# Moving the key-weight reads of layer 0's second output sweep to other weight tiles

## The chip, the cores and the metric

The kernel runs on one core of a Trainium2 chip. The metric is the device time of one execution in microseconds (us); it is the median of several runs. One further execution was recorded by the hardware profiler, and every row of a profile or trace below is from that one. Times inside the trace are counted from the start of its span.

## The reference

The program is a two-layer diffusion transformer with 256 tokens of `x` and 256 context tokens of `ctx`, model width 2048 and branch width 4096. All inputs are float32. Cut to what matters here:

```python
for i in range(2):
    shift, scale, gate = split(silu(c) @ ada_w[i] + ada_b[i], 3)          # modulation of x
    shift_c, scale_c, gate_c = split(silu(c_ctx) @ ada_w[i] + ada_b[i], 3) # modulation of ctx
    h  = rmsnorm(x,  norm_g[i]) * (1 + scale)   + shift
    hc = rmsnorm(xc, norm_g[i]) * (1 + scale_c) + shift_c
    y, yc = fourier_branch(h), fourier_branch(hc)      if i == 0
    y     = attention_branch(h, hc)                    if i == 1
    x  = x  + gate   * (y  @ w_out[i])
    xc = xc + gate_c * (yc @ w_out[i])                 # layer 0 only
return rmsnorm(x, final_g)
```

The stage of interest is the last product of layer 0, `y @ w_out[0]` for both token sets, a 512 x 4096 by 4096 x 2048 product. Beside it, and on other engines, the modulation of layer 1 (`silu(c) @ ada_w[1]`) and sums of squares of weights of layer 1 are computed.

## The kernel before, in words

**The output loop.** Lines 1028 to 1080 run `for i in range(32)`: two sweeps of 16 weight tiles, `sw = i // 16` and `kg = i % 16`. Sweep 0 makes the first half of the output columns, sweep 1 (the second sweep, tiles 16 to 31) the other half. For each i one 1 MB weight tile `raw` comes through SyncE's DMA queue (SP) from `in_wo`, three buffers deep. `split16` (L137, L138) makes of each half j of `raw` one fp16 pair `wf`: ScalarE (ACT) writes the high part (L137), VectorE (DVE) the remainder (L138). TensorE (PE) then runs 48 matmuls, three per block (L145, L146, L147): L145 and L146 read the high part, L147 the remainder that DVE wrote. Tiles with kg 14 and 15 go through `ws_split` (L66, L67) in place of it. PE begins the loop near 658 us of the trace, the first sweep ends near 826 and the second near 1000.

**The six weight buffers.** The pool with tag `ws` has six slots of 512 KB. The `wf` halves and the `wa` tiles of the modulation share them, so a new `wa` or `wf` takes the slot of whichever of them comes free, and its DMA or ACT instruction waits for the last reader of the tile that stood there.

**The modulation steps.** `next(ada)` (L784 to L795) is one step: a 512 KB tile `zr` of `ada_w` through SP's queue (L787, two buffers) and a 512 KB tile `wa` through POOL's queue (L790, in the `ws` pool), each multiplied on DVE with the activated condition `cb` and summed (L792). A step of a modulation with both token sets has two DVE passes for each tile, the first into a scratch tile `junk` and the second in place; one of x alone has one. `ada_rate` gives the number of steps per weight tile: two for i from 6 to 9 and from 17 to 25, none for 14, 15, 16 and from 28, else one.

**The pieces.** `scan_loads` (until i = 13) and `scan_loads1` read pieces of other weights on POOL's queue, two DMAs of 256 KB a piece (L834 for `in_wo`, L819 for `in_wkv`, the key weights of layer 1). `scan_sums` squares and sums what has been read, on ACT (L827). There are 16 key-weight pieces, 32 DMAs; all must be summed before `h1_bound` at i = 28 uses the sum.

**What sets the order.** The loop names the work, and each engine's instructions are then put in one fixed order when the program is built: an instruction that is ready early by the scheduler's reckoning may be put ahead of one named earlier. At run time every engine takes its instructions strictly in that order, so that one that waits holds up all behind it. DVE does the `wf` remainders, the modulation passes and, in the first sweep, `y_split0` (L894) in one such queue; POOL issues the `wa`, `in_wkv`, `in_wo` and `in_xT` transfers in one.

Of the kernel before, what the change touches and what calls it, by code (L numbers as in the profile page):

```python
# [32 lines left out]
def tile_dit(ctx: ExitStack, tc: tile.TileContext, a: dict, out: bass.AP):  # L33
# [10 lines left out]
    def psum():  # L44
        return pp.tile([P, 512], F32, tag="ps", name="ps")

    def raw(src, q=None):
        t = rawp.tile([P, D], F32, tag="raw", name="raw")
        n = src.shape[-1]
        last_dma[0] = (q or nc.sync).dma_start(t[:, :n], src).ins  # L50
        return t
# [3 lines left out]
    def act(dt=F32):  # L55
        return actp.tile([P, 512], dt, tag="act", name="act")
# [77 lines left out]
    def split16(t, i, up):  # L134
        w = wsp.tile([P, 2, 1024], F16, tag="ws", name="wf")
        src = t[:, i * 1024 : (i + 1) * 1024]
        last_cast[0] = S.activation(w[:, 0], src, AF.Copy, scale=up).ins  # L137
        last_sub[0] = V.scalar_tensor_tensor(w[:, 1], src, up, w[:, 0], op0=ALU.mult, op1=ALU.subtract).ins  # L138
        return w[:, 0], w[:, 1]

    def ws_split(t):
        return [half_split(t, i) for i in range(2)]
# [671 lines left out]
    def scan_loads1(n):  # L814
        for j in [next(scans1) for _ in range(n)]:
            for q in range(2):
                t = act()
                c = (j % 2 * 2 + q) * 512
                nc.gpsimd.dma_start(t, a["wkv"][j // 2][:, c : c + 512])  # L819
                c = j * 2 + q  # L820
                c += 80 if c < 28 else -28
                pend.append((t, scn[:, c : c + 1]))

    def scan_sums():
        while pend:
            t, c = pend.pop(0)
            S.activation(t, t, AF.Square, accum_out=c)  # L827

    def scan_loads(n):
        for j in [next(scans) for _ in range(n)]:  # L830
            for q in range(2):
                t = act()
                c = (j % 2 * 2 + q) * 512
                nc.gpsimd.dma_start(t, a["wo0"][j // 32, j % 32 // 2][:, c : c + 512])  # L834
                c = j * 2 + q - 64 * (j >= 40)
                pend.append((t, scn[:, c : c + 1]))
# [5 lines left out]
    def half_sum(sw):  # L842
        return [col_sum(scn[:, sw * 16 : sw * 16 + 64])] + [col_sum(scn[:, 80:108])] * (sw == 0)

    def half_scale(sw, sums_):
        x, up = sum_scale(sums_[0])
        if sw == 0:
            xy, uy = sum_scale(sums_[1])
            keep(ysc[:, 0:1].bitcast(I32), xy)
            keep(ysc[:, 1:2], uy)  # L850
        up_ = keep(ysc[:, 2 + 3 * sw : 3 + 3 * sw], up)
        both, dn = ysc[:, 3 + 3 * sw : 4 + 3 * sw], ysc[:, 4 + 3 * sw : 5 + 3 * sw]
        V.tensor_tensor(both, up_, ysc[:, 1:2], op=ALU.mult)
        V.tensor_scalar(dn.bitcast(I32), x, ysc[:, 0:1].bitcast(I32), -27.0 * 2**23, op0=ALU.add, op1=ALU.add)
        return up_, both, dn

    with tc.tile_pool(name="yp", reuse_waits="tile", bufs=32) as ypool:
# [23 lines left out]
        def y_split0(i):  # L881
            for j in range(2):
                k = i % 16 * 2 + j
                if k < 28:
                    if i < 16:
                        t = (ypool if k > 1 else actp).tile([P, 1024], F16, tag="y" if k > 1 else "act", name="y")
                        h, l, up = t[:, 0:512], t[:, 512:1024], ysc[:, 1:2]
                    else:
                        yy[i, j] = yy[i - 16, j]
                        continue  # L890
                else:
                    h, l, up = act(F32R), act(F32R), osc[i // 16][1]
                last_cast[0] = S.activation(h, ys[k], AF.Copy, scale=up).ins
                last_sub[0] = V.scalar_tensor_tensor(l, ys[k], up, h if k < 28 else h.bitcast(F32), op0=ALU.mult, op1=ALU.subtract).ins  # L894
                yy[i, j] = (h, l)
# [108 lines left out]
        def h1_bound():  # L1004
            m, c = h_bound(gs1, sh1, False), tiny(F32, 4, "t4")
            V.tensor_copy(c[:, 0:1], m)
            for i, q in ((2, slice(80, 108)), (3, slice(0, 4))):
                V.tensor_reduce(c[:, i : i + 1], scn[:, q], axis=AX.X, op=ALU.add)
            V.tensor_tensor(c[:, 1:2], c[:, 2:3], c[:, 3:4], op=ALU.add)
            nc.gpsimd.dma_start(hbd, c[:, 0:2])  # L1010
            hb1.append(act())
            nc.gpsimd.dma_start(hb1[0][:, 0:N], hbd.rearrange("(o p) c -> o (p c)", o=1).broadcast_to([P, N]))

        def h1_scale():
            v = hb1[0][:, 0:N].rearrange("p (n c) -> p c n", c=2)
            s = tiny()
            V.tensor_reduce(s, v[:, 0], axis=AX.X, op=ALU.max)
            x = exponent(s, 23)
            V.tensor_scalar(ek.bitcast(I32), x, -91.0, 2.0**23, op0=ALU.add, op1=ALU.mult)
            up = up_by(x, 268.0)  # L1020
            for d, t in ((gsz, gs1), (shz, sh1)):
                V.tensor_scalar(d, t, up, None, op0=ALU.mult)
            V.tensor_reduce(s, v[:, 1], axis=AX.X, op=ALU.add)
            V.tensor_scalar(kw, s, 2.0**-70, None, op0=ALU.max)
            V.tensor_scalar(kw.bitcast(I32), kw.bitcast(I32), 24, 23, op0=ALU.logical_shift_right, op1=ALU.logical_shift_left)
            V.tensor_scalar(upk.bitcast(I32), kw.bitcast(I32), -1.0, 204.0 * 2**23, op0=ALU.mult, op1=ALU.add)
            V.tensor_scalar(dnk.bitcast(I32), kw.bitcast(I32), ek.bitcast(I32), 2.0**23, op0=ALU.add, op1=ALU.max)
        for i in range(32):
            sw, kg = i // 16, i % 16
            if kg == 0:  # L1030
                o = [psum() for _ in range(8)]
            wr = raw(a["wo0"][sw, kg])
            w = [split16(wr, j, osc[sw][0]) for j in range(2)] if kg < 14 else ws_split(wr)
            with tc.issue_after(last_cast[0]):
                scan_sums()
            if i < 14:
                scan_loads({6: 1, 7: 1, 8: 1, 9: 1}.get(i, 2))
            scan_loads1({14: 1, 15: 2, 16: 1, 26: 2, 27: 1}.get(i, 1) if 14 <= i < 28 else 0)
            if i == 14:
                osc.append(half_scale(1, half_sum(1)))  # L1040
            if kg == 14:
                q = gt0[:, sw * 8 : sw * 8 + 8].rearrange("p k s -> p (k s)")
                V.tensor_scalar(q, q, osc[sw][2], None, op0=ALU.mult)
            if i in range(1, 31):
                with tc.issue_after(last_cast[0]), tc.issue_after(last_sub[0]):
                    y_split0(i + 1)
            elif i == 31:
                with tc.issue_after(last_sub[0]):
                    h1_scale()
                wr = raw(a["wkv"][0])  # L1050
                w0 = split16(wr, 0, upk)
            if i == 28:
                with tc.issue_after(last_sub[0]):
                    h1_bound()
            if kg >= 12:
                for k in range(sw * 8 + (kg - 12) * 2, sw * 8 + (kg - 12) * 2 + 2):
                    t = act()
                    nc.gpsimd.dma_start(t, a["xT"][:, k, :])
                    xin.append(t)
            with tc.issue_after(last_sub[0]):  # L1060
                for _ in range(ada_rate.get(i, 1)):
                    next(ada)
            edge = kg in (0, 15)
            for j, b in [(j, b) for b in range(8) for j in range(2)] if edge else [(j, b) for j in range(2) for b in range(8)]:
                q = slice(b * P, (b + 1) * P)
                last = i == 31 and (j, b) == (1, 7)
                if last:
                    sums.append(psum())
                    with tc.issue_after(e):
                        row_sums(0)  # L1070
                        row_sums(1)
                with tc.issue_after(st_end[0]) if last else nullcontext():
                    e = mm3(o[b], w[j][0][:, q], w[j][1][:, q], *yy[i, j], kg + j == 0, kg * 2 + j == NB - 1)
                if kg == 15 and j == 1:
                    evac0(sw * 8 + b, o[b])
# [646 lines left out]
```

## Time and profile before

| what | us |
|---|---|
| median of 3 runs | 1771.17 (1769.23 to 1772.79) |
| the profiled execution's own time | 1773.51 |
| its span in the trace | 1771.7 |
| TensorE busy | 1733.6 (98% of the span) |
| VectorE busy | 1405.9 (79%) |
| ScalarE busy | 1089.2 (61%) |
| GpSimd (POOL) busy | 333.8 (19%) |

A group row gives line, engine, operation and tiles, then the busy time and the mean duration in ns, then the idle time of that engine just before these instructions and what ended most of it. A row of the timeline gives the start, the duration and, in brackets, the idle time before it with its releaser. A matmul row lasts longer than the distance to the next one, since matmuls overlap; the rate is read from the starts. In a row of windows each engine has its busy time and, in brackets, its number of instructions; then follow the granted PE clock (1.00 is full), the busy share of the DMA engines and their GB/s.

### The profile page before, as it was taken

What the parts mean: (1) busy time and instruction counts of PE and PEld (TensorE: products, weight loads), DVE (VectorE), ACT (ScalarE), POOL (GpSimd) and SP (SyncE); (2) the same over time, 40 slices, a digit from 0 to 9 for tenths busy, and PEclk for the clock granted to TensorE, in tenths of its full rate; (3) what the DMA queues carried; (4) which work ended last, traced back from release to release, by engine and by line L of the source; (5) the groups of instructions that cost most, each with busy time, mean ns of one, the idle gap of its engine ahead of it and who ended that gap; (6) DMA issues with size and microseconds to landing.
All of it is one profiled execution on the core that took longest, in us unless ns stands there. A gap on an engine that the chain in (4) does not pass through costs nothing. (4 is left out here: it accounts for less than half of the span.)

```text
span 1771.7 us, 26606 instructions
## 1 busy us (share of the span) xinstructions
PE 1733.6 (98%) x9517; PEld 1188.4 (67%) x9517; DVE 1405.9 (79%) x2454; ACT 1089.2 (61%) x2069; POOL 333.8 (19%) x440
## 2 busy tenths in 40 slices
PE   6999999999999999999999999999999999999997
PEld 4679999544444444446434745788888888887886
DVE  5778889697777786886688695899999999997455
ACT  5545556477777755464324454688888878886343
POOL 0002111212222114121201001412303230234010
PEclk9999999999999999999999999999999999999999
DMA  9998999778988869985976532688987898888544
GB/s 393 418 355 242 288 273 255 288 285 318 330 306 318 313 222 374 364 293 201 367 270 210 170 130 72 190 198 205 216 214 204 216 221 195 206 211 270 190 166 143
DMA packets 229077, 447.29 MB, mean 252 GB/s; under 512 B 155888, under 2 KB 156288, under 8 KB 202064
## 3 DMA queue, kind: packets, MB, share of 16 engines
q1 hardware_dynamic: 182784, 331.93, 58.0%
q0 software_dynamic: 42016, 106.70, 19.4%
q10 hardware_dynamic: 4144, 6.95, 1.2%
q8 instruction: 75, 1.23, 0.3%
q14 instruction: 58, 0.48, 0.1%
HBM read 400.43 MB, written 12.59 MB: 233 GB/s over the span
## 5 line engine op out<-in xcount | busy, mean ns | idle before, releaser
L67 DVE TENSOR_TENSOR wl<-raw,wh 128x1024 fp32r<-128x1024 f32 x197 | 262.6, 1338 | 111.1 <-ACT wh L66 83.0
L66 ACT CAST wh<-raw 128x1024 fp32r<-128x1024 f32 x197 | 205.5, 1045 | 145.5 <-PE ps L146 103.2
L146 PE MATMUL ps<-act,wf 128*128 128x512 f16 x512 | 194.2, 379 | 0.0
L147 PE MATMUL ps<-act,wf 128*128 128x512 f16 x512 | 191.3, 379 | 0.0
L145 PE MATMUL ps<-act,wf 128*128 128x512 f16 x512 | 189.9, 379 | 0.6 <-ACT wf L137 0.3
L1386 PE MATMUL ps<-h,wh 128*128 128x512 f32 x512 | 185.9, 399 | 0.0
L147 PEld LDWEIGHTS <-wf 128*128 128x128 f16 x960 | 93.9, 98 | 118.1 <-DVE wf L138 4.5
L145 PE MATMUL ps<-y,wf 128*128 128x512 f16 x448 | 170.6, 381 | 0.8 <-ACT wf L137 0.8
L147 PE MATMUL ps<-y,wf 128*128 128x512 f16 x448 | 167.3, 381 | 4.0 <-DVE wf L138 4.0
L146 PE MATMUL ps<-y,wf 128*128 128x512 f16 x448 | 170.7, 381 | 0.0
L145 PEld LDWEIGHTS <-wf 128*128 128x128 f16 x960 | 93.8, 98 | 113.6 <-ACT wf L137 4.2
L146 PEld LDWEIGHTS <-wf 128*128 128x128 f16 x960 | 94.0, 98 | 109.5 <-issue 0.8
L137 ACT ACTIVATE wf<-raw,nrm 128x1024 f16<-128x1024 f32 x56 | 63.2, 1145 | 137.8 <-PE ps L147 82.1
L1388 PE MATMUL ps<-h,wl 128*128 128x256 f32 x512 | 139.2, 282 | 0.0
L138 DVE SCALAR_TENSOR_TENSOR wf<-raw,tn,wf 128x1024 f16<-128x1024 f32 x64 | 79.8, 1282 | 42.5 <-ACT wf L137 42.4
L1440 DVE SCALAR_TENSOR_TENSOR f<-p,sm,f 128x512 f16<-128x512 f32 x128 | 104.6, 837 | 8.6 <-ACT f L1439 8.4
L1427 ACT ACTIVATE p<-ps,mx 128x512 f32<-128x512 f32 x128 | 87.8, 688 | 36.7 <-DVE mx L1424 31.8
L790 POOL DMA_DIRECT2D wa<-in_adw x64 | 34.0, 532 | 404.7 <-DVE acc L792 163.5
L1386 PEld LDWEIGHTS ps<-h,wh 128*128 128x128 f32 x512 | 96.9, 189 | 19.1
L1439 ACT ACTIVATE f<-p,sm 128x512 f16<-128x512 f32 x128 | 87.7, 717 | 30.8 <-DMA ft<-f 12.4
L146 PE MATMUL ps<-wl,h 128*128 128x512 f32 x256 | 101.3, 396 | 0.0
L827 ACT ACTIVATE act<-act 128x512 f32<-128x512 f32 x160 | 98.4, 616 | 4.7 <-DMA act<-in_wo 4.4
(414 smaller groups left out, 4676.4 us busy)
## 6 DMA issues: line engine op xcount, KB each, us to landing
raw<-in_wz SPq DMA_DIRECT2D x64, 1024.0 KB, 5.6
raw<-in_awp SPq DMA_DIRECT2D x32, 1024.0 KB, 12.7
zr<-in_adw SPq DMA_DIRECT2D x64, 512.0 KB, 6.9
wa<-in_adw POOLq DMA_DIRECT2D x64, 512.0 KB, 6.3
act<-in_wo POOLq DMA_DIRECT2D x128, 256.0 KB, 7.8
raw<-in_wo SPq DMA_DIRECT2D x32, 1024.0 KB, 8.0
raw<-in_wq SPq DMA_DIRECT2D x32, 1024.0 KB, 5.2
raw<-in_wu SPq DMA_DIRECT2D x32, 1016.0 KB, 6.3
```

Source lines behind the costliest of these rows:

```text
L66: last_cast[0] = S.copy(h, src).ins
L67: last_sub[0] = eng.tensor_tensor(l, src, h.bitcast(F32), op=ALU.subtract).ins
L138: last_sub[0] = V.scalar_tensor_tensor(w[:, 1], src, up, w[:, 0], op0=ALU.mult, op1=ALU.subtract).ins
L145: PE.matmul(o, wh, xh, start=start, stop=False)
L146: PE.matmul(o, wh, xl, start=False, stop=False)
L147: return PE.matmul(o, wl, xh, start=False, stop=stop).ins
L827: S.activation(t, t, AF.Square, accum_out=c)
L1386: PE.matmul(o[0], wh[:, q], hx1[k], start=k == 0, stop=k == KT - 1)
L1388: PE.matmul(o[0][:, 0:N], wl[:, q], hx1[k][:, 0:N], start=False, stop=False)
L1427: S.activation(pt[tb], so[tb], AF.Exp, bias=mx[:, tb : tb + 1], scale=-1.0, accum_out=sm[:, tb : tb + 1])
L1439: S.activation(f[:, 0:512], pt[tb], AF.Copy, scale=sm[:, tb : tb + 1])
L1440: V.scalar_tensor_tensor(f[:, 512:1024], pt[tb], sm[:, tb : tb + 1], f[:, 0:512], op0=ALU.mult, op1=ALU.subtract)
```

## The change

One line in the loop, the number of key-weight pieces that weight tile i reads ahead:

```diff
@@ -1035,7 +1035,7 @@
                 scan_sums()
             if i < 14:
                 scan_loads({6: 1, 7: 1, 8: 1, 9: 1}.get(i, 2))
-            scan_loads1({14: 1, 15: 2, 16: 1, 26: 2, 27: 1}.get(i, 1) if 14 <= i < 28 else 0)
+            scan_loads1({10: 1, 11: 1, 14: 2, 15: 2, 16: 2, 26: 2, 27: 2}.get(i, 1 - i % 2) if 10 <= i < 28 and i not in (12, 13) else 0)
             if i == 14:
                 osc.append(half_scale(1, half_sum(1)))
```

Before, tiles 14 and 16 name one piece, 15 two, each of 17 to 25 one, 26 two and 27 one. After, tiles 10 and 11 name one, 14, 15, 16, 26 and 27 two, the even tiles 18 to 24 one, and the odd tiles 17 to 25 as well as 12 and 13 none. It is 16 pieces both times. No instruction is added or removed; the order on the engines and the slots of the `ws` pool change.

The first place is POOL's queue around the end of the first sweep. Rows are DMAs with the number of equal ones in a row; `in_adw` is the modulation weight, `in_wkv` the key weight.

```order
 L790 DMA wa<-in_adw 128x1024 x2
-L819 DMA act<-in_wkv 128x512 x22
-L790 DMA wa<-in_adw 128x1024
-L819 DMA act<-in_wkv 128x512 x3
-L790 DMA wa<-in_adw 128x1024
-L819 DMA act<-in_wkv 128x512
-L790 DMA wa<-in_adw 128x1024 x16
+L819 DMA act<-in_wkv 128x512 x20
+L790 DMA wa<-in_adw 128x1024 x18
```

The burst of key-weight DMAs after the sweep's end is 20 long instead of 22, and the four that stood between the first `wa` DMAs of the second sweep are gone: the 18 `wa` DMAs follow one another. Six key-weight DMAs moved ahead, among the `in_wo` reads of tiles 10 and 11 and the reads at tile 14; four of them stand ahead of the third and all later `wa` DMAs of that stretch (`wa_7735` and `wa_7741`, whose passes stand ahead of tile 8's first half on DVE, are the first).

The second place is DVE's queue around weight tile 20, whose first half is `wf_8882` before and `wf_8896` after, and whose second half is `wf_8885` before. Before:

```order
-L792 ISA zr_8826,acc_4144<-zr_8826,cb_8056 128x1024
-L792 ISA acc_4144 128x1
-L138 SCALAR_TENSOR_TENSOR wf_8882<-raw_8880,nrm_101,wf_8882 128x1024
-L792 ISA junk_4143,acc_4144<-wa_8746,cb_8056 128x1024
-L792 ISA acc_4144 128x1
-L792 ISA wa_8746,acc_4144<-wa_8746,cb_8056 128x1024
```

After:

```order
+L792 ISA zr_8840,acc_4144<-zr_8840,cb_8060 128x1024
+L792 ISA acc_4144 128x1
+L792 ISA junk_4143,acc_4144<-wa_8764,cb_8060 128x1024
+L792 ISA acc_4144 128x1
+L792 ISA wa_8764,acc_4144<-wa_8764,cb_8060 128x1024
+L792 ISA acc_4144 128x1
+L792 ISA junk_4143,acc_4144<-zr_8832,cb_8060 128x1024
+L792 ISA acc_4144 128x1
+L138 SCALAR_TENSOR_TENSOR wf_8896<-raw_8894,nrm_101,wf_8896 128x1024
+L792 ISA zr_8832,acc_4144<-zr_8832,cb_8060 128x1024
```

The first `wa` of the burst (`wa_8746` before, `wa_8764` after, the first of 16 and of 18 in POOL's rows above) now has both of its passes ahead of the first half of tile 20; before it had them behind it.

The third place is POOL's queue at the modulation steps that tiles 21 to 23 name, with the semaphores that each `wa` DMA waits for (`DMASW` is an earlier DMA of the same queue, `DVE`, `PE` and `Activation` are engines). Before:

```order
L790 DMA wa_8977<-in_adw 128x1024 [waits DMASW7_49,DVE_49]
L790 DMA wa_8984<-in_adw 128x1024 [waits DMASW0_49,PE_49,Activation_49]
L790 DMA wa_9053<-in_adw 128x1024 [waits DMASW1_49,DVE_49]
L790 DMA wa_9060<-in_adw 128x1024 [waits DMASW2_49,DVE_49]
L790 DMA wa_9129<-in_adw 128x1024 [waits DMASW3_49,DVE_49]
L790 DMA wa_9136<-in_adw 128x1024 [waits DMASW4_49,DVE_49]
```

After, at the same places of the queue:

```order
L790 DMA wa_8985<-in_adw 128x1024 [waits DMASW7_49,PE_49,Activation_49]
L790 DMA wa_8992<-in_adw 128x1024 [waits DMASW0_49,PE_49,Activation_49]
L790 DMA wa_9059<-in_adw 128x1024 [waits DMASW1_49,DVE_49,PE_49]
L790 DMA wa_9066<-in_adw 128x1024 [waits DMASW2_49,DVE_49,PE_49]
L790 DMA wa_9131<-in_adw 128x1024 [waits DMASW3_49,DVE_49,PE_49]
L790 DMA wa_9138<-in_adw 128x1024 [waits DMASW4_49,DVE_49,PE_49]
```

Before, five of the six take the slot of another `wa` tile and wait for its DVE pass. After, all six take the slot of a `wf` half and wait for the matmuls (PE) that read it, those of the weight tile that named it.

## The prediction

> **What bounds the kernel now.** I read the page first: TensorE is busy for 98% of the span, so only what makes TensorE wait, or slows its clock, can be won back.
>
> ```profile
> PE 1733.6 (98%) x9517; PEld 1188.4 (67%) x9517; DVE 1405.9 (79%) x2454; ACT 1089.2 (61%) x2069; POOL 333.8 (19%) x440
> ...
> L147 PE MATMUL ps<-y,wf 128*128 128x512 f16 x448 | 167.3, 381 | 4.0 <-DVE wf L138 4.0
> ```
>
> The second row already names the one wait of size in the changed stage: a matmul on the remainder half waited 4.0 us for VectorE. The view of TensorE's waits between 655 and 1010 us confirms that there is only one such wait, and a smaller one at the boundary of the sweeps:
>
> ```profile
> PE ps L147 <- DVE wf L138: 4.0, 1, 4.0
> PE ps L145 <- ACT wf L137: 0.8, 1, 0.8
> ```
>
> TensorE's timeline then shows where it is and what follows it.
>
> ```profile
> 923.98 0.39 PE L147 MATMUL ps<-y,wf 128*128 128x512 f16 x1 [4.05 <-DVE wf L138]
> ...
> 924.76 0.63 PE L147 MATMUL ps<-y,wf 128*128 128x512 f16 x1
> 925.19 0.63 PE L145 MATMUL ps<-y,wf 128*128 128x512 f16 x1
> ...
> 928.05 0.38 PE L146 MATMUL ps<-y,wf 128*128 128x512 f16 x1
> 928.27 0.38 PE L147 MATMUL ps<-y,wf 128*128 128x512 f16 x1
> ...
> 928.91 0.38 PE L147 MATMUL ps<-y,wf 128*128 128x512 f16 x1
> ```
>
> The wait begins at 923.98 - 4.05 = 919.93, at the start of weight tile 25. After it the starts lie 0.43 us apart (924.76 to 925.19), until 928.05; then they lie (928.91 - 928.05) / 4 = 0.215 us apart. From 923.98 to 928.27 there are 12 distances, 4.29 us where 12 x 0.215 = 2.58 would do: 1.71 us more. The windows agree that it is the clock:
>
> ```profile
> 910.00:920.00 10.00, 9.93 (x47) 4.29 (x44) 8.16 (x13) 0.33 (x1) 1.59 (x3) 1.00 0.76 270
> 920.00:930.00 10.00, 6.02 (x21) 2.37 (x22) 8.51 (x13) 3.42 (x6) 0.53 (x1) 0.83 0.65 237
> ```
>
> So the stall costs 4.05 + 1.71 = **5.76 us**, and this is the most that the change can win in this loop but for the 0.8 us.
>
> VectorE's timeline says why.
>
> ```profile
> 898.66 1.22 DVE L792 CUSTOM_DVE_ANT_0 wa<-wa,cb 128x1024 f32<-128x1024 f32 x1 [1.74 <-DMA wa<-in_adw]
> 899.81 0.08 DVE L792 DVE_READ_ACCUMULATOR2_ANT acc<- 128x1 f32 x1
> ...
> 906.73 1.28 DVE L138 SCALAR_TENSOR_TENSOR wf<-raw,nrm,wf 128x1024 f16<-128x1024 f32 x1
> 910.06 1.23 DVE L792 CUSTOM_DVE_ANT_0 wa<-wa,cb 128x1024 f32<-128x1024 f32 x1 [2.04 <-DMA wa<-in_adw]
> ...
> 921.49 1.23 DVE L792 CUSTOM_DVE_ANT_0 wa<-wa,cb 128x1024 f32<-128x1024 f32 x1 [3.27 <-DMA wa<-in_adw]
> ...
> 922.64 1.28 DVE L138 SCALAR_TENSOR_TENSOR wf<-raw,nrm,wf 128x1024 f16<-128x1024 f32 x1
> ```
>
> The remainder of tile 25 (922.64) stood in VectorE's queue behind a modulation pass that waited 3.27 us for its `wa`. The waits grow, 1.74, 2.04, 3.27, about 11.4 us apart. One pass takes 899.81 - 898.66 = 1.15 us and one remainder about 1.2, so a weight tile with two steps gives VectorE 6 x 1.15 + 2 x 1.2 = 9.3 us of work, against 48 x 0.215 = 10.3 us on TensorE. VectorE has time enough; the `wa` transfers come too late. POOL's timeline closes the circle:
>
> ```profile
> 852.62 0.54 POOL L819 DMA_DIRECT2D act<-in_wkv  x1 [0.30 <-issue]
> 853.62 0.54 POOL L819 DMA_DIRECT2D act<-in_wkv  x1 [0.46 <-issue]
> 855.11 0.53 POOL L790 DMA_DIRECT2D wa<-in_adw  x1 [0.95 <-DMA act<-in_wkv]
> ...
> 861.89 0.54 POOL L790 DMA_DIRECT2D wa<-in_adw  x1 [1.55 <-DMA act<-in_wkv]
> 862.41 0.54 POOL L819 DMA_DIRECT2D act<-in_wkv  x1
> 863.10 0.53 POOL L790 DMA_DIRECT2D wa<-in_adw  x1 [0.15 <-issue]
> ...
> 901.33 0.53 POOL L790 DMA_DIRECT2D wa<-in_adw  x1 [0.62 <-DVE acc L792]
> 911.59 0.53 POOL L790 DMA_DIRECT2D wa<-in_adw  x1 [9.73 <-DVE acc L792]
> 912.74 0.53 POOL L790 DMA_DIRECT2D wa<-in_adw  x1 [0.61 <-DVE acc L792]
> ```
>
> A `wa` DMA issued at 901.33 was used at 910.06, and one issued at 912.74 at 921.49: each 8.7 us later, the moment it landed. Each waited for VectorE to release the slot of an earlier `wa`, and VectorE waits for it in turn: a loop of landing 8.7 us and 2.7 us of passes, 11.4 us, against TensorE's 10.3. It loses 1.1 us a tile; the margin of tile 24 was 919.93 - 10.3 - (906.73 + 1.28) = 1.6 us, and at tile 25 it is gone.
>
> **The change part by part.** *Number of instructions:* the same on every engine, so no busy time is won or lost: 0.
>
> *The four key-weight DMAs that leave the places between the `wa` DMAs.* The burst is two shorter, so the first `wa` stands where the 21st key-weight DMA stood, 852.62 in place of 855.11, the second at 853.62 in place of 861.89, the third near 855.1 in place of 863.10. The early tiles' `wa` come 2.5 to 8 us sooner.
>
> *The slots.* By the built program the `wa` DMAs of the steps that tiles 21 to 23 name wait for matmuls on `wf` halves in place of VectorE's passes. TensorE reads the last of a half in the middle and at the end of a tile, so these transfers start about a tile, 10 us, before their pass. That opens the loop of 11.4 us. The `wa` that made the stall (the second of tile 24) still waits for a VectorE pass, but for one that itself runs on time, and its own pass now stands behind both halves of tile 25 and no longer ahead of the first.
>
> ```profile
> DMA to landing us min/median/max: 3.9/7.9/10.7
> ...
> DMA to landing us min/median/max: 4.7/6.7/10.7
> ```
>
> These are the landing times of the `wa` and then of the `zr` tiles between 845 and 945 us. Ten us of lead covers a `wa` landing of 7.9 and just misses the longest of 10.7.
>
> *VectorE's new order.* The first `wa` of the burst now has two passes ahead of tile 20's first half. Tile 20 starts at 919.5 - 5 x 10.35 = 867.8, and by the new order of TensorE ten matmuls (2.15 us) come before the first that reads the remainder, so the deadline is 869.9. With issue at 852.62 and the longest landing, 10.7, the passes start at 863.3, and four instructions of 4.6 us later the remainder is done at about 868. Margin 2 us. Stepping on in the same way I find margins of 1.2 to 1.5 us at tiles 21 and 22, and about 1 us at 23 to 26. Nothing is hidden with much to spare.
>
> *What is late next: `zr`.* Two buffers, one reused each half tile. In the new order five VectorE instructions (5.8 us) lie between the release of a `zr` buffer and the pass on the tile that takes it; with the 1.0 us that VectorE has spare per tile, a landing of up to 6.7 us costs nothing, and one of L us puts VectorE L - 6.7 behind at every tile. The median is just 6.7. By bounds: at 4.7 nothing, at 10.7 four us a tile. I take the median, so no steady loss, but with margins of 1 us a landing above the median at one tile will show. The nearest row for such a late half is the 0.8 us wait at the sweeps' boundary, which cost no clock in the rows after it; I charge **0.8 us** once (ends 0 and 4).
>
> *The six key-weight DMAs that move ahead.* Four of them (1 MB) stand ahead of `wa` transfers that VectorE needs around tile 8:
>
> ```profile
> 700.00:720.00 20.00, 20.00 (x94) 9.11 (x93) 15.17 (x22) 10.60 (x23) 8.58 (x16) 1.00 1.02 397
> 720.00:740.00 20.00, 20.00 (x95) 9.02 (x93) 17.71 (x27) 9.50 (x16) 2.65 (x5) 1.00 0.95 342
> ...
> 723.89 1.23 DVE L792 CUSTOM_DVE_ANT_0 junk<-wa,cb 128x1024 f32<-128x1024 f32 x1 [1.87 <-DMA wa<-in_adw]
> ...
> 733.81 1.28 DVE L138 SCALAR_TENSOR_TENSOR wf<-raw,nrm,wf 128x1024 f16<-128x1024 f32 x1
> ```
>
> The DMA engines are full there; 1 MB at 397 GB/s is 2.6 us. The first half of tile 8 is done at 735.1, and tile 8 starts at 867.8 - 12 x 10.35 - the 0.8 us, less some 2 us for the two longer L66 tiles, = about 741 (estimate), so 6 us of cover hold 2.6: cost 0, ends 0 and 1.5. ScalarE's squares move with them; it is busy half the time there (9.50 of 20 us): 0.
>
> *Sum*, against the profiled execution of 1773.51 (span 1771.7): -5.76 + 0.8 = **-5.0 us**. That execution lies 2.3 us above the median of the runs, a usual distance for their spread of 3.6, and the stall is fixed by the order of the program, so I carry the same difference to the median: 1771.17 - 5.0 = **1766.2**. All later stages start when TensorE ends this one and are bound by it, so the gain stays.
>
> [...] The rows above show the clock lost after a 4.05 us wait and not after 0.8 us. [...]
>
> **The rivals.** *A: the stall stays in part or moves.* The `zr` landing, or a `wa` landing over 10 us, takes the place of the wait removed. For it: the margins of 1 us, the `zr` median at the break-even, and waits of VectorE for DMAs at five places of this stretch. Against it: the `wa` loop was the one that lost time at each tile, and `zr` caused none of the last three waits above. If 2 to 5 us of the 5.76 are lost again in one or more waits, the time is 1767.7 to 1771.
>
> *B, slower: `zr` becomes the steady bound.* If `zr` lands in 8.4 us in the new arrangement (halfway from the median to the longest), VectorE loses 1.7 us a tile, at the tiles 20 to 25 10.2 us, less 1 us of margin: 9.2 us of waits, each of 1.7 us and so nearer to the 0.8 us that cost no clock than to the 4.05: 1765.4 + 9.2 = 1774.6. From there on, L of 8.4 and more, the kernel is slower; at 10.7 it would be 4.0 x 6 - 1 = 23 us, 1788. For it: with four `wa` in flight earlier, `zr` shares the engines with more transfers. Against it: the bytes per tile after 863 are the same as before.
>
> *C: no effect, since the reads are where they were.* The key-weight DMAs do not stand at the tiles that name them: the built program has them in one burst both times. Were only the names moved, the time would stay at 1771.2. Against it: slots and places really differ. This is in A's chance.
>
> **How the numbers follow.** Forecast (stall gone, at most 2.3 us of waits left): 0.57, time 1763.8 to 1767.6, around **1766.2**. A and C: 0.28, 1767.7 to 1774.5. B: 0.15, above 1774.7. A measurement of this kernel can tell 0.2%, 3.5 us, from no change, so faster means under 1767.6: 0.57; within: 0.28; slower: 0.15. The range leaves out B's upper half and little below: 1763.5 to 1775.5; the lower end is the whole 5.76 won with 1.9 us of the runs' spread.
>
> **What would show it.** Right: no wait of TensorE for L138 near 920 us, windows of clock 1.00 between 920 and 930, POOL's `wa` rows after 880 us released by PE, the first `wa` after the burst issued near 852.6. Wrong: waits of VectorE for `zr` that grow from tile to tile, or a TensorE wait for L138 at tile 20 near 870 us, which would mean that the burst did not get shorter in time, or one at tile 8, which would mean that the moved reads delayed `wa` by more than 6 us.

## The result and the profile after

The changed kernel takes **1766.56 us** (median of 20 runs, 1763.6 to 1776.01), the kernel before 1772.48 us (20 runs, 1766.05 to 1776.51). The ratio is 0.9973, with a 95% interval of 0.9962 to 0.9984: faster by 0.27%, some 4.8 us; the two medians alone lie 5.9 us apart, the two means 4.3. The forecast was 5.0 us. The profiled execution of the changed kernel has a span of 1767.8 us, that of before 1771.7.

The view of TensorE's waits between 655 and 1010 us, after:

```profile
PE ps L145 <- ACT wf L137: 0.8, 1, 0.8
PE ps L147 <- DVE wf L138: 0.4, 1, 0.4
```

The wait of 4.05 us is gone; one of 0.4 us has come, and the one at the sweeps' boundary has stayed. The windows show that the clock's loss went with the wait:

```profile
900.00:920.00 20.00, 20.00 (x94) 9.11 (x93) 19.48 (x31) 5.77 (x8) 1.59 (x3) 1.00 0.92 305
920.00:940.00 20.00, 20.00 (x95) 9.08 (x93) 19.88 (x32) 7.87 (x13) 1.58 (x3) 1.00 0.82 289
```

TensorE is busy all 40 us at full clock. VectorE, 16 to 17 us of 20 busy before, is now busy 19.5 us and more, as less of its time goes into waits. Its timeline (idle time before an instruction in brackets, with the releaser) shows which of them are left:

```profile
862.60 1.22 DVE L792 CUSTOM_DVE_ANT_0 junk<-wa,cb 128x1024 f32<-128x1024 f32 x1 [4.41 <-DMA wa<-in_adw]
...
866.16 1.28 DVE L138 SCALAR_TENSOR_TENSOR wf<-raw,nrm,wf 128x1024 f16<-128x1024 f32 x1
...
887.04 1.23 DVE L792 CUSTOM_DVE_ANT_0 zr<-zr,cb 128x1024 f32<-128x1024 f32 x1 [2.27 <-DMA zr<-in_adw]
...
888.30 1.28 DVE L138 SCALAR_TENSOR_TENSOR wf<-raw,nrm,wf 128x1024 f16<-128x1024 f32 x1
...
906.49 1.23 DVE L792 CUSTOM_DVE_ANT_0 zr<-zr,cb 128x1024 f32<-128x1024 f32 x1 [0.53 <-DMA zr<-in_adw]
...
916.91 1.28 DVE L138 SCALAR_TENSOR_TENSOR wf<-raw,nrm,wf 128x1024 f16<-128x1024 f32 x1
```

No pass waits for a `wa` after 862.60. The first half of tile 20 is done at 866.16 + 1.28 = 867.4, and that of tile 25 at 918.2. What is left is `zr`. The wait of 2.27 us at 887.04 holds up the remainder of tile 22 (888.30), and that is TensorE's 0.4 us. POOL's timeline shows why `wa` comes in time:

```profile
852.11 0.53 POOL L790 DMA_DIRECT2D wa<-in_adw  x1 [0.51 <-DMA act<-in_wkv]
853.41 0.53 POOL L790 DMA_DIRECT2D wa<-in_adw  x1 [0.76 <-DMA act<-in_wkv]
854.74 0.53 POOL L790 DMA_DIRECT2D wa<-in_adw  x1 [0.80 <-DMA act<-in_wkv]
...
883.24 0.53 POOL L790 DMA_DIRECT2D wa<-in_adw  x1 [4.40 <-PE ps L147]
...
894.21 0.53 POOL L790 DMA_DIRECT2D wa<-in_adw  x1 [5.26 <-PE ps L147]
899.39 0.53 POOL L790 DMA_DIRECT2D wa<-in_adw  x1 [4.65 <-PE ps L147]
904.57 0.53 POOL L790 DMA_DIRECT2D wa<-in_adw  x1 [4.65 <-PE ps L147]
```

The first three stand at 852 to 855 us, and from 894 to 905 one `wa` is released by TensorE's matmuls every 5.2 us, half a weight tile, where before two came together every 11.4 us after a VectorE pass. Landing has become shorter for both in this pair: between 860 and 930 us the median went from 7.9 to 7.0 us for `wa` and from 6.6 to 5.6 for `zr`. For `wa` that says little, since two more profiles of before (e6 and e7 below) have 6.6 and 6.9; for `zr` they have 7.2 both times. These are the landing times (minimum, median, maximum) of `wa` and then `zr` from 860 to 930 us, after:

```profile
DMA to landing us min/median/max: 4.2/7.0/8.7
...
DMA to landing us min/median/max: 4.2/5.6/8.0
```

The start of the first matmul behind the loop (L145 on `hz`) marks what the loop gave. Before, it is

```profile
1007.98 0.38 PE L145 MATMUL ps<-wf,hz 128*128 128x512 f16 x1
```

and after

```profile
1002.36 0.38 PE L145 MATMUL ps<-wf,hz 128*128 128x512 f16 x1
```

From the loop's first matmul (658.16 and 657.86) that is 349.82 and 344.50 us, 5.3 us apart: the 5.76 less the 0.43. In this pair of executions layer 1 gives some 1.5 us of it back by longer waits (L1457 and L1449 wait 5.3 us in all before, 6.8 after), so the spans are only 3.9 apart; the ratio of the 20 runs each says 4.8.

### The profile page after: what moved, and what is told of

It is laid out like the page before. It is cut to its first block, busy times and chain, and to the rows that moved or that the text cites. A ratio compares the mean times of both kernels' runs of the same rounds, so it can differ in the third digit from the quotient of the medians.

```text
span 1767.8 us, 26608 instructions
## 1 busy us (share of the span) xinstructions
PE 1732.2 (98%) x9517; PEld 1187.7 (67%) x9517; DVE 1406.6 (80%) x2454; ACT 1090.5 (62%) x2069; POOL 331.9 (19%) x440
## 5 line engine op out<-in xcount | busy, mean ns | idle before, releaser
L145 PE MATMUL ps<-act,wf 128*128 128x512 f16 x512 | 189.8, 379 | 0.6 <-ACT wf L137 0.2
L145 PE MATMUL ps<-y,wf 128*128 128x512 f16 x448 | 169.8, 379 | 0.8 <-ACT wf L137 0.8
L145 PEld LDWEIGHTS <-wf 128*128 128x128 f16 x960 | 93.7, 98 | 113.3 <-ACT wf L137 4.2
L137 ACT ACTIVATE wf<-raw,nrm 128x1024 f16<-128x1024 f32 x56 | 63.4, 1145 | 137.1 <-DVE acc L792 68.5
L138 DVE SCALAR_TENSOR_TENSOR wf<-raw,tn,wf 128x1024 f16<-128x1024 f32 x64 | 79.8, 1281 | 42.0 <-ACT wf L137 41.9
```

The source lines that it names most:

```text
L145: PE.matmul(o, wh, xh, start=start, stop=False)
```

## The experiments

The theory: VectorE's queue is late when a modulation transfer, with its landing and the passes between release and reuse, takes longer round than TensorE's 10.3 us a tile; the change wins because `wa` takes slots that TensorE releases. The rivals: that the place of the `wa` DMAs behind the key-weight burst decides; that only the odd tiles matter; that the profiled execution was by chance.

The length of the loop, from the first L145 on `y` to the first on `hz`, sums up every profiled run. The sum in the third column adds the waits for L138 and the clock's loss to the 343.92 us of the run e8, which has neither.

| run | loop, us | waits for L138 and clock loss, us |
|---|---|---|
| before | 349.82 | 4.05 + 1.71, sum 349.7 |
| e6, before again | 346.76 | 0.74 + 1.76, sum 346.4 |
| e7, before a third time | 350.31 | 2.23 + 2.13 + 1.7, sum 350.0 |
| e1, even tiles only | 345.69 | 1.04 + 0.43, sum 345.4 |
| e2, one early piece | 349.89 | 1.14 + 2.88 + 1.5, sum 349.4 |
| e3, two early pieces | 347.66 | 0.45 + 2.96, sum 347.3 |
| e5, second part alone | 350.17 | 0.64 + 0.45 + 2.96 + 1.7, sum 349.7 |
| changed | 344.50 | 0.43, sum 344.4 |
| e8, changed again | 343.92 | none |

### e1: no piece on the odd tiles

```diff
-            scan_loads1({14: 1, 15: 2, 16: 1, 26: 2, 27: 1}.get(i, 1) if 14 <= i < 28 else 0)
+            scan_loads1({14: 1, 15: 2, 16: 1, 18: 1, 20: 1, 22: 1, 24: 1, 26: 4, 27: 4}.get(i, 0))
```

> Only the names move inside the second sweep: one piece on each even tile 18 to 24, none on the odd ones, four on 26 and 27, while tiles 14 to 16 keep 1, 2, 1 and tiles 10 and 11 have none. TensorE's, POOL's and SP's orders come out as before, VectorE's up to tile 27 too. Theory (the wa transfers and their slots make the stall): the wait of 4.05 us for L138 near 924 us and the slow matmuls after it come back, 5 to 6.5 us together, time as before. Rival (what counts is that no piece falls on an odd tile with two steps): the wait goes, 4 to 6 us faster than before.

Measured: 1770.61 us (12 runs), ratio to before 1.0000 (0.9986 to 1.0013). TensorE's waits in its profile:

```profile
921.36 0.39 PE L147 MATMUL ps<-y,wf 128*128 128x512 f16 x1 [1.04 <-DVE wf L138]
...
942.68 0.39 PE L147 MATMUL ps<-y,wf 128*128 128x512 f16 x1 [0.43 <-DVE wf L138]
```

The time is that of before, so the rival falls: taking the pieces off the odd tiles alone changes nothing that can be measured. (The expectation has the reason: TensorE's, POOL's and SP's orders come out as before.) But the theory's 5 to 6.5 us did not come back in this execution: the waits are 1.5 us, at tiles 25 and 27. The runs e6 and e7 below were made for this.

### e2 and e3: parts of the early pieces

e2 has one early piece and two each at 14 to 16; e3 has both early pieces and 14 to 16 as before.

```diff
-            scan_loads1({14: 1, 15: 2, 16: 1, 26: 2, 27: 1}.get(i, 1) if 14 <= i < 28 else 0)
+            scan_loads1({10: 1, 14: 2, 15: 2, 16: 2, 18: 2, 20: 2, 22: 2, 24: 2, 26: 1}.get(i, 0))  # e2
+            scan_loads1({10: 1, 11: 1, 14: 1, 15: 2, 16: 1, 26: 1, **{j: 1 for j in range(17, 26)}}.get(i, 0))  # e3
```

> One piece at tile 10, two each at 14, 15, 16, the rest later. POOL's queue has the 18 wa DMAs after the sweep's end in one row, as in the changed kernel, behind 22 key-weight DMAs instead of 20; but the wa tiles of tiles 21 to 24 take slots of other wa tiles, as before. Theory (slots close a loop of landing and passes, 11.4 us against TensorE's 10.3): VectorE still waits for wa between 880 and 925 us, by waits that grow from tile to tile, but starts some 3 us better off: TensorE waits 0 to 2.5 us near tile 25, time 3 to 6 us under before. Rival (the four DMAs between the wa DMAs made them late, nothing else): no wait of VectorE for wa after 880, no wait of TensorE there, as the changed kernel.

> One piece each at tiles 10 and 11, tiles 14 to 16 as before (1, 2, 1), 17 to 26 one each: the first part of the change alone. POOL's 18 wa DMAs stand in one row behind 22 key-weight DMAs, the slots of the wa tiles are those of other wa tiles. Theory: as for the kernel with one early piece, waits of VectorE for wa that grow between 880 and 925, TensorE waiting 0 to 2.5 us near tile 25. Rival: no wait for wa after 880, none of TensorE.

Measured: e2 1772.82 us, ratio 1.0014 (1.0000 to 1.0029); e3 1774.65 us, ratio 1.0014 (0.9999 to 1.0030). Both have the 18 `wa` DMAs in one row, and neither gains. VectorE's waits in e2:

```profile
896.89 1.23 DVE L792 CUSTOM_DVE_ANT_0 wa<-wa,cb 128x1024 f32<-128x1024 f32 x1 [1.52 <-DMA wa<-in_adw]
...
908.93 1.23 DVE L792 CUSTOM_DVE_ANT_0 wa<-wa,cb 128x1024 f32<-128x1024 f32 x1 [2.58 <-DMA wa<-in_adw]
...
923.64 1.22 DVE L792 CUSTOM_DVE_ANT_0 junk<-zr,cb 128x1024 f32<-128x1024 f32 x1 [2.92 <-DMA zr<-in_adw]
...
933.92 1.23 DVE L792 CUSTOM_DVE_ANT_0 junk<-zr,cb 128x1024 f32<-128x1024 f32 x1 [1.90 <-DMA zr<-in_adw]
```

The waits for `wa` at 896.89 and 908.93 are what the theory asked for and the rival forbade. The rival, that the four DMAs between the `wa` DMAs made them late and nothing else, falls. What these two runs leave untested is the shorter burst: their first `wa` is issued at 855.27 and 855.70 us, no sooner than before (855.11), while the changed kernel's is at 852.11. The theory had two things wrong as well. In e3 the waits for `wa` did not grow but fell, 2.12, 1.27 and 0.70 us. And I expected 3 to 6 us under before, and then `zr` came late where `wa` had done, in e2 by 2.92 and 1.90 us. TensorE paid at tile 27 in place of tile 25:

```profile
926.13 0.39 PE L147 MATMUL ps<-y,wf 128*128 128x512 f16 x1 [1.14 <-DVE wf L138]
...
944.73 0.61 PE L147 MATMUL ps<-y,wf 128*128 128x512 f16 x1 [2.88 <-DVE wf L138]
```

The median landing of `zr` was 7.3 us in e2 and 7.4 in e3, over the 6.7 that the prediction worked out for the changed kernel's order. Why the wait came at tile 27 is shown under e6 and e7.

### e4: wa in two slots of its own

```diff
-    wsp = ctx.enter_context(tc.tile_pool(name="ws", bufs=6))
+    wsp = ctx.enter_context(tc.tile_pool(name="ws", bufs=4))
...
-                                wf = wsp.tile([P, 1024], F32, tag="ws", name="wa")
+                                wf = adat.tile([P, 1024], F32, tag="wa", name="wa", bufs=2)
```

> The pieces of the changed kernel, but wa has two slots of its own and the other weight tiles share four instead of six, so that every wa takes the slot of a wa. Other stages have fewer buffers too, so only the second sweep is read. Theory (loop): one slot's turn is landing 7.6, issue 0.6 and 3.5 to 4.6 of passes, 11.7 to 12.8 us, against TensorE's 10.3: VectorE waits for wa at nearly every tile from 20 on and TensorE loses 1.4 to 2.5 us a tile over 6 to 8 tiles, less a lead of 3 to 4: 5 to 16 us of waits for L138 between 860 and 945. Rival (only the place in POOL's queue counts; wa stands in one row behind the burst as in the changed kernel): at most 1 us of waits. On the clock: waits of 1 to 3 us each show whether they cost clock as the one of 4.05 did.

Measured: 1835.16 us (one run), with longer waits in other stages, whose pool is smaller too (7.0 us at L995, for instance, where before has 0.4). In the second sweep there is no wait for L138 at all, against the theory's 5 to 16 us. TensorE began this sweep late, though, after a wait of 6.59 us for ScalarE's high part (L137) at 843.78, so that its tiles are not timed as in the changed kernel. VectorE's waits from 890 to 925 us:

```profile
899.59 1.23 DVE L792 CUSTOM_DVE_ANT_0 junk<-wa,cb 128x1024 f32<-128x1024 f32 x1 [1.58 <-DMA wa<-in_adw]
...
901.98 1.23 DVE L792 CUSTOM_DVE_ANT_0 wa<-wa,cb 128x1024 f32<-128x1024 f32 x1 [1.06 <-DMA wa<-in_adw]
...
922.14 1.22 DVE L792 CUSTOM_DVE_ANT_0 wa<-wa,cb 128x1024 f32<-128x1024 f32 x1 [2.74 <-DMA wa<-in_adw]
```

and the landing times of its `wa` from 860 to 930 us:

```profile
DMA to landing us min/median/max: 3.8/5.1/8.7
```

The mistake was to put 7.6 us, near the landing of before (7.9), into the sum for this kernel. At a median of 5.1 a turn is 5.1 + 0.6 + 3.5 to 4.6 = 9.2 to 10.3 us, within TensorE's 10.3, and only single long landings make VectorE wait. So a slot released by VectorE was not late by itself here; the slot and the landing together made the turn. Why `wa` lands sooner here was not found.

### e5: the second part alone

```diff
-            scan_loads1({14: 1, 15: 2, 16: 1, 26: 2, 27: 1}.get(i, 1) if 14 <= i < 28 else 0)
+            scan_loads1({14: 2, 15: 2, 16: 2, 18: 1, 20: 1, 22: 1, 24: 1, 26: 3, 27: 3}.get(i, 0))
```

> Two pieces each at tiles 14, 15 and 16 and none at 10 and 11, the rest on even tiles from 18 and on 26 and 27: the second part of the change alone. POOL has one wa, two key-weight DMAs and then 17 wa in a row after the burst of 22; the slots of the wa tiles are those of other wa tiles. Theory (the gain needs the wa transfers to be released by TensorE's reads of wf halves): VectorE waits for wa or, where wa comes in time, for zr, and TensorE waits 1.5 to 6 us for L138 between 880 and 950; time within 0.2% of before. Rival (the pieces at 14 to 16 are the part that matters): no wait of TensorE over 0.5 us there, 4 to 6 us under before.

Measured: 1774.26 us, ratio 1.0013 (1.0003 to 1.0024), as the theory had it. TensorE waited 0.64, 0.45 and 2.96 us, the last again at tile 27. VectorE had waited for `wa` once (2.19 us at 898.55), and its last waits ahead of these halves were again for `zr`, 2.47 us at 923.73 and 2.60 at 934.70. With e2 and e3 it follows that none of the parts tried wins alone: in e2, e3 and e5 the `wa` slots are the old ones, released by VectorE, and the time is that of before or 0.1% above. Of the kernels run, only the one with both parts has the other slots.

### e6, e7 and e8: the same kernels once more

No edit.

> The kernel before, profiled once more. The order is the same, so a wait that is fixed by the order alone returns with 4 us near 924; if it depends on how long the transfers take in that execution, the waits for L138 between 880 and 950 come out anywhere from 1 to 6 us, at the same tiles 25 and 27.

> As the kernel before profiled again: waits for L138 of 1 to 6 us in all at tiles 25 and 27, and slow matmuls only after a wait near 3 us or above.

> The changed kernel, profiled once more. Theory: the wa DMAs of the second sweep are released by TensorE again, VectorE has no wait for wa after 880, and TensorE waits 0 to 1.5 us for L138 between 860 and 950. Rival (the first profile was a lucky execution): 2 us and more.

Measured, profiled executions: e6 1774.53 us, e7 1775.3 us, e8 1767.41 us. TensorE's waits in e6:

```profile
921.65 0.39 PE L147 MATMUL ps<-y,wf 128*128 128x512 f16 x1 [0.74 <-DVE wf L138]
...
944.31 0.39 PE L147 MATMUL ps<-y,wf 128*128 128x512 f16 x1 [1.76 <-DVE wf L138]
```

and in e7:

```profile
924.14 0.39 PE L147 MATMUL ps<-y,wf 128*128 128x512 f16 x1 [2.23 <-DVE wf L138]
...
947.17 0.39 PE L147 MATMUL ps<-y,wf 128*128 128x512 f16 x1 [2.13 <-DVE wf L138]
...
948.19 0.63 PE L147 MATMUL ps<-y,wf 128*128 128x512 f16 x1
948.62 0.63 PE L145 MATMUL ps<-y,wf 128*128 128x512 f16 x1
```

With the order of before the stall was there in each of these executions, but not of one size: with the clock's loss it was 5.8, 2.5 and 6.1 us, and 1.5 in e1, whose order is the same that far. Nor is it in one place: the first profile has it at tile 25 alone, the other three at tiles 25 and 27. Their landing times differ.

The two places have two causes. At tile 25 a pass waited for `wa` (2.35 us in e6, 3.44 in e7). At tile 27 the pass ahead waited for `zr`, which SP issued when VectorE had released its buffer (SP's row and VectorE's row in e6):

```profile
926.25 1.47 SPq L787 DMA_DIRECT2D zr<-in_adw  x2
```

```profile
933.51 1.22 DVE L792 CUSTOM_DVE_ANT_0 junk<-zr,cb 128x1024 f32<-128x1024 f32 x1 [2.48 <-DMA zr<-in_adw]
```

VectorE was ready at 933.51 - 2.48 = 931.03, 4.8 us after the issue, and this transfer took 7.2 us. From there VectorE had work all but without a pause until the remainder at tile 27 was done, too late. All seven profiles with the old slots (before, e1, e2, e3, e5, e6, e7) have this place with the same 4.8 us, and VectorE waits there for 1.13 to 2.84 us. VectorE's order in the changed kernel has no such place: the shortest time that it leaves a `zr` after 875 us is 5.7 us, and the `zr` issued at 926.59 is first used at 937.14. In e6 and e7 the larger part of the stall (1.76 of 2.5 us and 3.8 of 6.1) stands at tile 27. In e8 TensorE has no wait for L138 and VectorE none for `wa` after 880; its waits for `zr` are 0.45, 0.28, 1.05 and 0.42 us. The mean loop of the three profiles of before is 348.96 us, that of the two of the changed kernel 344.21: 4.75 us, beside the 4.8 of the runs (3.9 if e1 is counted with before). Both loops of the changed kernel are shorter than all those with the old slots, so its first profile was not by chance.

### e9 and e10: half the bytes

Only the transfer is halved; the passes read the half twice. In e9 the edit falls on `wa` (`f == 1`), in e10 on `zr` (`f == 0`).

```diff
-                                nc.gpsimd.dma_start(wf, a["adw"][i, kh, fg][:, q])
+                                nc.gpsimd.dma_start(wf[:, 0:512], a["adw"][i, kh, fg][:, q][:, 0:512])
...
-    V.tensor_tensor_reduce(junk if s == 0 and i < 3 else wf, wf, cb[:, s], 1.0, ...)
+    V.tensor_tensor_reduce(junk.rearrange("p (u k) -> p u k", u=2), wf[:, None, 0:512].broadcast_to([P, 2, 512]), cb[:, s].rearrange("p (u k) -> p u k", u=2), 1.0, ...) if f == 1 else V.tensor_tensor_reduce(junk if s == 0 and i < 3 else wf, wf, cb[:, s], 1.0, ...)
```

> The kernel before with wa transfers of 256 KB in place of 512: only the left half of each wa tile is read, and its passes use it twice, so the second halves of those modulation rows are left out and VectorE has as much to do. The built order differs: 26 key-weight DMAs in one burst ahead of the second sweep's wa (the first wa later than in any other kernel here), half of the wa slots those of other wa tiles. Theory (landing plus passes has to stay under TensorE's 10.3 us a tile): wa lands in 4 to 6 us and VectorE has no wait for wa over 1 us after 880, TensorE waits 0 to 1.5 us for L138 in 880 to 950. Rival (the place behind the burst decides): waits for wa of 2 us and more, TensorE 3 us and more near 870 or 924.

> The kernel before with zr transfers of 256 KB in place of 512, the left half used twice in the same way (the second halves left out). POOL's order is nearly that of before, half of the wa slots are those of other wa tiles. Theory: zr lands in 4 to 6 us, so VectorE's waits for zr near 923 and 934 and TensorE's wait at tile 27 near 944 go, while waits for wa of 1 to 2.5 us may stay; TensorE waits 0 to 1.5 us in 880 to 950. Rival (the late halves come from wa and the burst alone): TensorE waits 2 us and more at tiles 25 and 27.

Measured: e9 1772.77 us, e10 1766.39 us, one run each beside 1771.24 for before; the loop is 345.83 and 344.06 us. In e9, POOL's first `wa` after the burst and VectorE's waits ahead of the two remainders that TensorE waited for:

```profile
858.89 0.54 POOL L790 DMA_DIRECT2D wa<-in_adw  x1 [0.94 <-DMA act<-in_wkv]
```

```profile
891.63 1.23 DVE L792 CUSTOM_DVE_ANT_0 zr<-zr,cb 128x1024 f32<-128x1024 f32 x1 [2.19 <-DMA zr<-in_adw]
...
903.30 1.23 DVE L792 CUSTOM_DVE_ANT_0 zr<-zr,cb 128x1024 f32<-128x1024 f32 x1 [0.73 <-DMA zr<-in_adw]
```

The first `wa` came at 858.89, 3.8 us later than before and 6.8 later than in the changed kernel, and still no pass waited for a `wa` after 880 us; TensorE waited 0.31 and 0.54 us for L138, both times behind `zr`. With a landing of 4.3 us (median) the `wa` loop is short enough even behind this longer burst. In e10 TensorE has no wait for L138 at all, though a pass waited 2.50 us for its `wa` at 905.77: both waits, at tile 25 and at tile 27, are gone. The built order of these two differs from that of before, and in both `wa` and `zr` land sooner (medians of 4.3 and 5.4 us in e9, 5.1 and 5.6 in e10); e10 also issues its first `wa` at 849.83. So they go with the reading that shorter landings remove nearly all of the stall, but they do not part `wa` from `zr`, nor landing from order. One run each decides nothing on the time: the loop of e9 is as short as that of e1, and its run is the slower one of the pair.

## Why the prediction was right, point by point

*The stall and what can be won.* Right in place and in kind for the execution that it read; 5.3 us of 5.76 were won in the profiled pair. What was wrong is the sentence that the stall "is fixed by the order of the program": its size was 1.5 to 6.1 us in four executions, and three of them had part of it at tile 27, behind `zr`. The prediction put all of the stall down to `wa` and had no term for that part. (In its own profile VectorE's wait of 1.48 us for `zr` at 934.84 stood at the same place, without cost, since TensorE was late by the stall at tile 25.) The forecast took one execution's 5.76 for all; the mean of before's three profiles above the changed kernel's two, 4.75, is smaller, and nearness to the measured 4.8 is luck of about a microsecond. So is that of the time itself, 1766.2 against 1766.56: the median of before that it starts from, 1771.17 of 3 runs, came out 1.3 us higher with 20.

*The burst.* Predicted 852.62, 853.62 and 855.1 for the first three `wa`; measured 852.11, 853.41 and 854.74. Right. What coming sooner is worth by itself was not run: e2 and e3 have the `wa` DMAs in one row, but their first is no sooner than before.

*The slots.* Right: of POOL's ten `wa` rows from 857 to 905 us, TensorE releases six, and no pass waits for a `wa` once the first has landed, in either profile. All seven profiles with the old slots have a wait for `wa` of 2.0 us or more after 895 us. After 905 us the rows are no longer TensorE's, against the sign that the prediction named. That the slots took away the wait at tile 25 is what the traces say; that they alone carried the gain is not shown, since every run that has them also has the shorter burst and the VectorE order that gives `zr` more time at tile 27. The steady loss of 1.1 us a tile in the loop of before was too simple: it holds for landings of 8.7, not for the 6.4 to 6.9 (medians) of e1, e6 and e7.

*VectorE's new order.* The first half of tile 20 was predicted for about 868 and was done at 867.4. What the prediction did not see in this order is that it also takes away the short turn of `zr` at tile 27.

*What is late next.* `zr`, as predicted: the 0.8 us charged once was 0.43 in one execution and nothing in the other. The five instructions reckoned at 5.8 us between release and reuse measured 5.7. Rival B had its condition, a landing above 6.7 us, not in the changed kernel (5.6 and 5.8) but in e2, e3 and e5 (7.3 to 7.4), and also in the kernel before with e6 and e7 (7.2) and in e1 (7.1). That `zr` would land sooner in the changed kernel was not foreseen. By the prediction's own sum, 6.7 - 5.6, it left about a microsecond more at each tile, which is luck.

*The early reads.* Cost nothing: there is no wait of TensorE between 700 and 800 us in any of these runs.

*The clock after a wait.* The trace of before has clock lost after a wait of 4.05 us and none after one of 0.77 (826.09, where the next starts are 826.31, 826.53 and 826.75). Between the two it has no wait in this loop, and how a wait that is only shortened would act was open. e7 has a wait of 2.13 us that cost clock (0.91 from 940 to 960 us).

Open stays what makes landings differ by 1 to 2 us between kernels and executions with the same bytes, and so why e2, e3 and e5 have `wa` at 5.4 to 5.7 but `zr` at 7.3, and the changed kernel 7.0 and 5.6. Open too is how the gain divides between the slots of `wa`, the shorter burst and the turn of `zr`.

## What to carry to other kernels

Where a DMA waits for the slot of a tile that is read by an engine with a queue of other work (here VectorE, where tile 25's remainder stood behind a pass that waited 3.27 us), add landing, issue and the instructions between release and reuse, and compare the sum with the period of the bounding engine. Before, it was longer in the profiled execution, 11.4 us against 10.3, and the waits grew from 1.74 to 3.27 us; slots that the bounding engine itself releases are one thing to try: the changed kernel has them, and no wait for `wa` after 862.60. Do this sum for every queue that is fed in this way, and at its shortest turn: here `zr` was late at a single turn of 4.8 us. A schedule's small table can act through the slots and the orders that are built from it and not through the places that it names, so read the built order and its waits first. A stall that hangs on landing times can have a size of its own in each execution (here 1.5 to 6.1 us in four): profile the kernel more than once before pricing it.

## What the runs showed of the hardware

In these runs the length of a wait did not tell whether it cost clock. Waits for L138 of 1.76, 2.23 and 2.96 us (e6, e7, e3) were followed by matmuls at full rate, and waits of 2.13, 2.88, 2.96 and 4.05 us (e7, e2, e5, before) by 3.0 to 3.6 us of matmuls at or near half rate (0.43 us from start to start in place of 0.215), 1.5 to 1.7 us lost each. My expectation for e7, slow matmuls only after a wait near 3 us or above, was wrong. The same kernel did both within 23 us. The windows of e3 and e7 with the tile-27 waits, granted clock in the third column from the right:

```profile
940.00:960.00 20.00, 17.04 (x80) 7.50 (x79) 19.93 (x33) 9.20 (x13) 0.00 (x0) 1.00 0.52 188
```

```profile
940.00:960.00 20.00, 17.87 (x76) 7.58 (x75) 19.90 (x32) 11.20 (x19) 0.25 (x1) 0.91 0.55 196
```

The first is e3 (2.96 us waited, clock 1.00), the second e7 (2.13 us, clock 0.91). What else than the length tells them apart is not shown.
